# Attention products padded to 128 contracted rows, and transposes alternated with products of 64 columns, in a two-layer float32 encoder

## The chip, the cores and the metric

The kernel runs on one core of one Trainium2 chip. The metric is the device time of one execution in microseconds (us), median of several runs; lower is better. Engines are named as the profile names them: PE is TensorE's matmul, PEld its weight load, DVE is VectorE, ACT is ScalarE, POOL is GpSimd, SP is SyncE, which issues the transfers.

## What is computed

512 tokens of width 1024 in float32 go through two layers and a final RMS norm. Each layer is: norm, token mixer, residual; norm, squared-ReLU MLP of width 4096, residual; then a gated embedding added to the residual.

```python
# layer 0: three groups of five heads of width 64, windows of dilation 1, 4, 16;
# per head: s = q k^T * 64**-0.5, masked softmax, o = p v; the groups mixed by their log-sum-exp
x = x + dilated_window_mixer(rmsnorm(x), ...)
# layer 1: latent attention, 16 heads; q and k of width 64 + 32 (rotated), v of width 64
x = x + latent_attention_mixer(rmsnorm(x), ...)     # full softmax over 512 keys
# after each mixer
x = x + relu(rmsnorm(x) @ w_up)**2 @ w_down
x = x + sigmoid(rmsnorm(x) @ w_gate) * (p @ w_proj)
```

## The kernel before, in words

Activations lie transposed, features on the partitions and tokens on the free axis, tokens sorted by their residue mod 4, so that each class is one tile of 128 tokens. Every float32 product runs as three float32r passes over operands split in two, hi.hi + lo.hi + hi.lo; `mm3` (lines 162 to 164) issues the three, and `split` (169, 170) makes the two parts, hi on ACT and lo on DVE. Weights come in blocks of up to 128x1024, two or three blocks ahead, split in the same way (137, 138).

**Layer 0, attention.** `attnA(i)` (411 to 588) takes head i of each of the three groups. Groups 1 and 2 share one product of 128 rows, with zeros put into the halves of `kh` and `kl_` (319 to 322). Group 0 has q hi over q lo in `qq`, and k hi twice in `kk`, so that one product of 128 rows (line 448) gives hi.hi + lo.hi; the third pass, hi.lo, is line 449, which contracts only the 64 rows of `kl`. `values0` (523 to 533) multiplies v of group 0: 128-column products with [v hi | v lo] (529), 64-column ones (531), and at the end line 532, a product of 64 rows of zeros over 512 columns whose only use is to close the accumulation. `weave` puts the steps of the next head's projections (`qkv`), or of the output projection (`woA1`), among those of `attnA`. After the last head lines 611 to 619 add the last k-tiles of the output projection, per output tile five products of 512 columns, of which line 617 contracts 64 rows; then come the residual (284), and the norm's split (172, 173) and squares, with POOL adding the squares (235). The MLP's first products follow and need each of those splits.

**Layer 1, latent attention.** After the projections (717 to 785) the main loop (931 to 958) runs over 64 steps s; a step is one tile of 128 queries of one head. `where(s)` gives the pair of heads p, the pair of query tiles tp, the head j and the tile i. In a step: `normal(s+3)` scales the exponentials (reciprocal on DVE, product on POOL, 857), `turn(s)` transposes the softmax in four 128x128 transposes (864) and splits it, `scores(s+4)` makes three products over 96 rows (847, shown as 162 to 164) and then minimum (849) and exponential (850), and `values(s-3)` makes two products of 128 stationary columns (883: [v hi | v lo] over p hi) and two of 64 (882 or 886: v hi over p lo), with the output's copy, sum and split (894, 895, 897) at every fourth step. Projections of later heads (`prepK`, `prepQ`, `groupQ`, `groupV`) and half of the output projection (`woB(0)`) are spread over the steps. The bank, tile and order of each instruction come from a scheduler that follows the program's order as far as slots are free: 8 banks of PSUM, 24 slots for 128x1024 tiles (`unit`), 18 for 128x512 (`half`).

`q` of a pair lies in two tiles taken anew for each pair (824), `k` in two pairs of tiles held from line 785 on; only their first 96 partitions are written and read.

Of the kernel before, what the change touches and what calls it, by code (L numbers as in the profile page):

```python
"""Two-layer hybrid encoder trunk (dilated window attention, latent attention) on one core.

Activations live transposed, features on partitions and tokens on the free axis, the tokens
sorted by their residue mod 4, so that each residue class is one tile of 128 tokens.
Every float32 product runs as three float32r passes over operands split exactly in two:
hi = round12(v), lo = v - hi, and a.b = hi.hi + lo.hi + hi.lo.
"""
# [16 lines left out]
P = 128  # L24
S = 512
# [17 lines left out]
def _schedule():  # L43
    """Weight blocks in the order of use: (name, index) -> columns per partition."""
    out = []
    for i in range(GH):
        out += [(("qkv", i, b), 1024) for b in range(4)]
        if i == 0:
            out += [(("v0", b), n * 320) for b, n in enumerate((3, 3, 2))]
    out += [(("woA1", m), 768) for m in range(8)]  # L50
    out += [(("woA2", h), 1024) for h in range(2)]
    out += _mlp_blocks(0)
    out += [(("win", b), 832) for b in range(4)]
    out += [((n, 0), c) for n, c in (("uq", 768), ("ukv", 512))]
    for g in range(1, 4):
        out += [((n, g), c) for n, c in (("uq", 768), ("ukv", 512))]
    out += [(("woB", h, b), 1024) for h in range(2) for b in range(4)]
    out += _mlp_blocks(1)
    return out
# [18 lines left out]
def trunk(ctx: ExitStack, tc: tile.TileContext, xT, pT, cols, mask, tabs, wts, out):  # L78
# [37 lines left out]
    # ---- weights: fetched and split a few blocks before their use  # L116
# [9 lines left out]
    def fetch(key, pieces=1):  # L126
        """Brings a block in and splits it; by pieces, a step per piece."""
# [20 lines left out]
    # ---- activations and constants  # L148
# [11 lines left out]
    def mm3(out_, l, r, first, last):  # L160
        """out += l.T @ r, l and r (hi, lo) pairs."""
        T.matmul(out_, l[0], r[0], start=first, stop=False)  # L162
        T.matmul(out_, l[1], r[0], start=False, stop=False)  # L163
        T.matmul(out_, l[0], r[1], start=False, stop=last)  # L164

    def split(hi, lo, src, gain=None):
        """hi, lo <- src (times a column), exactly."""
# [8 lines left out]
    # ---- norms  # L176
    def preload(func):
        """Has ScalarE's table of func in place ahead of its first use."""
        t = small(1)
        A.activation(t, ones[:, :1], func)  # L180

    def rsqrt(ss, n, width):
        """1/sqrt(ss/width + eps) of n columns, a tile or one by one: three Newton steps."""
# [22 lines left out]
    def spread(r, n):  # L206
        """The n columns of r along the free axis of a bank, on all partitions."""
# [5 lines left out]
    class Norm:  # L213
        """Takes finished tiles of x: the gained tiles split, and the tokens' sums of squares."""
# [33 lines left out]
        def columns(self, blocks=False):  # L248
            """rstd of the tokens as [128, 4] columns, by classes, and then by blocks of 128."""
# [11 lines left out]
        def row(self):  # L261
            """The columns along the free axis, on all partitions."""
            rb = half()
            A.copy(rb, spread(self.r, NT))
            return rb

    def blocked(t, done=False):
        """t by blocks of 128 tokens (done: already laid out so), of each class 32."""
# [5 lines left out]
    def dense(key, kt, rhs, n=1, c0=0):  # L274
        """An output tile [128, 512] in PSUM, weights stationary."""
# [10 lines left out]
    def rope(E, t, heads, half, c0, s0):  # L286
        """Rotates the leading 2*half columns of each head of t [128, 4, heads, w] in place."""
# [15 lines left out]
    def weave(main, side, n_side, lead=0):  # L303
        """Emits side's n_side steps among those of main, which yields how far side should be (from the lead on)."""
# [13 lines left out]
    # ---- layer 0: dilated window attention  # L318
    kh, kl_ = unit(F32R, (P, NT, 256)), unit(F32R, (P, NT, 256))
    for t in (kh, kl_):  # L320
        G.memset(fl(t[0:64, :, 128:256]), 0.0)
        G.memset(fl(t[64:128, :, 0:128]), 0.0)

# [21 lines left out]
    # the tokens by blocks of 128: of each class the 32 from 32b  # L345
# [20 lines left out]
    def qkv(i):  # L366
        """q, k (roped) and v of head i of each group, tokens on partitions; not the v of group 0."""
# [44 lines left out]
    def attnA(i):  # L412
        qk, v12 = proj.pop(i)
        # q and k of head i of each group, transposed and split
# [9 lines left out]
        # group 0: queries by sixteens of each class, keys by thirty-twos  # L424
        qq, kk, kl = unit(F32R), half(F32R), half(F32R)
# [12 lines left out]
        # of both parts of the keys (group 0; groups 1 and 2), by query tiles: the least score, negated, and the sum  # L438
        st = small(16).rearrange("p (g t c) -> p g t c", g=2, t=NT)

        def scores(t):
            """Groups 1 and 2 for the class t, group 0 for 128 tokens from 128t+64 on (cyclically)."""
# [6 lines left out]
            T.matmul(ps[:, 256:], qq[:64, qs], kt(kl[:64]), start=False, stop=True)  # L449
# [9 lines left out]
        def mix():  # L459
            """The factors of both parts, by classes."""  # L460
# [30 lines left out]
        def turn0(ts):  # L491
            """Group 0 of query tiles; slots of the keys' block b: 2b, 2b + 1."""
# [7 lines left out]
        def turn(tp):  # L500
            """Groups 1 and 2 of two classes."""
# [7 lines left out]
        def values(tp):  # L509
            """o of groups 1 and 2 of two classes."""  # L510
# [12 lines left out]
        def values0():  # L523
            """o of group 0: [v hi | v lo] over p hi, v hi over p lo."""
# [3 lines left out]
            for b in (1, 3, 2, 0):  # L528
                T.matmul(out_(po, b), v0[b][:, i].rearrange("p z c -> p (z c)"), ph[:, 2 * b:2 * b + 2],
                         start=b == 1, stop=False)  # L530
                T.matmul(out_(po[:64], b), v0[b][:, i, 0, :], pl[:, 2 * b:2 * b + 2], start=False, stop=False)
            T.matmul(po, kh[:64, 0, P:], kh[:64, :, P:], start=False, stop=True)
# [29 lines left out]
        # group 0 by classes again, with its factors  # L562
# [29 lines left out]
    def woA1():  # L592
        """The output projection of the heads before the last ones."""
# [17 lines left out]
    for m in range(KD):  # L611
# [5 lines left out]
        T.matmul(ps, w[1][:64, c + P:c + 256], oA[7][0][:64], start=False, stop=True)  # L617
# [3 lines left out]
    # ---- squared-ReLU MLP, then the gated per-layer embedding  # L621
# [92 lines left out]
    # ---- layer 1: latent attention  # L714
# [6 lines left out]
    for tp in range(2):  # L721
# [10 lines left out]
        # the latent norms: columns (q, kv) of two token tiles, the scores' factor in q's, negated  # L732
# [16 lines left out]
    # the rotated key part in columns 64..95 of a slab of 128  # L749
# [11 lines left out]
    def groupQ(g):  # L761
        """q of four heads, roped, tokens on partitions; a step per token tile, then per product of the rotation."""
# [22 lines left out]
    kts = [(unit(F32R), unit(F32R)) for _ in range(2)]  # L785
# [6 lines left out]
    def groupV(g):  # L792
        """v of four heads, tokens on partitions: [hi | lo] of each head."""
# [15 lines left out]
    qts = {}  # L809

    def prepK(p):
        """k of a pair of heads, transposed and split; a step per head."""
# [9 lines left out]
    def prepQ(p):  # L822
        """q of a pair of heads, transposed and split; a step per head."""
        qh, ql = unit(F32R), unit(F32R)
        qts[p] = qh, ql
# [10 lines left out]
    def where(s):  # L836
        """Pair of heads, pair of token tiles, head of the pair, tile of the pair."""
        return s // 8, s // 2 % 2, s // 4 % 2, s % 2

    def scores(s):  # L840
        """A token tile of queries of a head against all keys: the exponentials and their sum."""
        p, tp, j, i = where(s)
        (qh, ql), (kh, kl) = qts[p], kts[p % 2]
# [3 lines left out]
        mm3(ps, (qh[:QW, c], ql[:QW, c]), (kh[:QW, js], kl[:QW, js]), True, True)  # L847
# [11 lines left out]
    def turn(s):  # L859
        """The softmax transposed and split."""  # L860
        e, i = es.pop(s)[0], s % 2
        pt = bank()
        for c in range(4):
            T.transpose(pt[:, tok(c)], e[:, tok(c)], ident)  # L864
        if i == 0:
# [4 lines left out]
    def values(s):  # L870
        """Half of the keys into the output of two token tiles of a head."""
# [6 lines left out]
        v = [vs[p // 2][c // 2][:, c % 2, h * P:(h + 1) * P] for c in range(4)]  # L878
        for c in (2 * i, 2 * i + 1):
            if c == 3:  # L880
                for d in (2, 3):
                    T.matmul(o_[:64], v[d][:, :64], pl[:, d, :], start=False, stop=False)
            T.matmul(o_, v[c], ph[:, c, :], start=c == 0, stop=c == 3)  # L883
            if c == 1:
                for d in (0, 1):
                    T.matmul(o_[:64], v[d][:, :64], pl[:, d, :], start=False, stop=False)
        if i == 1:
            del pts[s // 2]
# [42 lines left out]
    for s in range(N + 3):  # L931
        if s + 3 < N:
            scaled = normal(s + 3)
        if s < N:
            turn(s)
        if s + LA < N:
            scores(s + LA)
        if 3 <= s:
            values(s - 3)
# [25 lines left out]
    # ---- last gate and the final norm, half of the tokens after the other  # L965
# [4 lines left out]
    def finish(h, acc, xg):  # L970
        """The final norm of half h: the tokens' sums of squares, row, products and stores."""
# [16 lines left out]
    def evac(h, b, ps, acc, xg):  # L988
        """Gate, residual and squares of two tiles, by tiles where ps is two banks; then their final gain."""
# [65 lines left out]
def _arrange(inp):  # L1055
    """Lays the inputs out for the chip; the constants depend on shapes alone."""
# [6 lines left out]
    def feat(a):  # L1063
        """[S, n*128] -> [128, n*S], tokens permuted."""
# [9 lines left out]
    def tiles(w, rows, cols_):  # L1074
        """[rows, cols] of w as [128, rows/128, cols]."""
# [12 lines left out]
    def one(w, k0, m):  # L1088
        """An output tile, eight k-tiles: [128, 8, 128]."""
# [37 lines left out]
    # rope tables of the permuted tokens, cos and sin of either width  # L1127
# [6 lines left out]
    # group 0: query tile t holds the sixteens 2t+1 and 2t+2 (mod 8) of each class, by class;  # L1134
    # the keys' blocks are t and t+1 (0 and 3), each by classes
# [11 lines left out]
    # groups 1 and 2: the keys of the query's class  # L1147
# [25 lines left out]
```

## Time and profile before

| | us |
|---|---|
| median of 3 runs (lowest, highest) | 1290.01 (1289.76, 1292.22) |
| span of the profiled execution | 1287.7 |
| PE busy | 1260.0 (98%) |
| PEld busy | 1055.5 (82%) |
| DVE busy | 737.8 (57%) |
| ACT busy | 587.2 (46%) |
| POOL busy | 139.5 (11%) |
| mean granted TensorE clock | 0.994 |

The profile gives the span, from the first instruction to the last, of one execution; its own time is not listed apart from the runs, whose median is 2.3 us above the span. Busy times of PE are modelled from pipelined products, so what one product costs is read from one start to the next, and not from its duration. Layer 0's attention lies at about 20 to 247 us, the first MLP and gate up to about 655, the latent attention up to about 862, the second MLP and the end behind it.

### The profile page before, as it was taken

How to read it: one execution, taken by the hardware profiler on the slowest of the kernel's cores; microseconds unless marked ns; L12 is line 12 of the kernel's file. 1: busy time of each engine (PE TensorE's matmuls, PEld its weight loads, DVE VectorE, ACT ScalarE, POOL GpSimd, SP SyncE). 2: the span in 40 equal slices, each digit the busy share in tenths (PEclk: the TensorE clock that was granted, in tenths of full speed). 3: DMA queues.
4: the chain of work that ended last, by engine and by line, in shares of the span. 5: the costliest groups of instructions: out<-in, count | busy, mean ns of one | idle time of the engine just before them, and what ended most of it. 6: DMA issues, size and time to landing. Idle time of an engine off the chain costs nothing.

```text
span 1287.7 us, 16148 instructions
## 1 busy us (share of the span) xinstructions
PE 1260.0 (98%) x6229; PEld 1055.5 (82%) x6229; DVE 737.8 (57%) x1236; ACT 587.2 (46%) x967; POOL 139.5 (11%) x173
## 2 busy tenths in 40 slices
PE   8999999999999999999999999999999999999997
PEld 6877778688888888888888888888888888888896
DVE  7566666744343343454778999864434434335477
ACT  5555564543132231344458887754313313224464
POOL 5000000200000000011123443220000000000200
PEclk9999999899999999999999999999999999999998
DMA  6211112222222222232220010122332232223342
GB/s 222 67 66 66 58 50 94 79 84 96 98 98 98 98 98 98 98 112 88 87 74 26 30 40 27 34 84 96 99 98 98 98 98 96 92 96 110 99 155 108
DMA packets 34348, 113.18 MB, mean 88 GB/s; under 512 B 4064, under 2 KB 4832, under 8 KB 34272
## 3 DMA queue, kind: packets, MB, share of 16 engines
q1 hardware_dynamic: 34272, 112.15, 25.8%
q8 instruction: 49, 0.80, 0.3%
q14 instruction: 27, 0.22, 0.1%
HBM read 110.04 MB, written 2.10 MB: 87 GB/s over the span
## 4 chain that ended last, share of the span: by engine, by line
PE 85%; DVE 8%; ACT 5%; issue 1%; DMA 1%; POOL 0%; DVEq 0%; SPq 0%; ACTq 0%
PE ps L162 26%; PE ps L164 26%; PE ps L163 26%; PE ps L864 2%; DVE wl L138 1%; DVE u L173 1%; DVE x L284 1%; ACT u L169 1%; DVE u L170 1%; PE ps L883 1%; ACT h L850 1%; ACT h L169 1%; ACT wh L137 1%; PE ps L257 1%; PE ps L449 0%
## 5 line engine op out<-in xcount | busy, mean ns | idle before, releaser
L162 PE MATMUL ps<-u,wh 128*128 128x512 f32 (+1 forms) x1256 | 477.4, 380 | 2.1 <-ACT u L172 2.1
L164 PE MATMUL ps<-u,wh 128*128 128x512 f32 (+1 forms) x1256 | 476.8, 380 | 2.5 <-DVE u L173 2.5
L163 PE MATMUL ps<-u,wl 128*128 128x512 f32 (+1 forms) x1256 | 475.9, 379 | 0.0
L137 ACT CAST wh<-wr 128x1024 fp32r<-128x1024 f32 (+4 forms) x213 | 215.5, 1013 | 524.1 <-PE ps L164 454.1
L138 DVE TENSOR_TENSOR wl<-wr,wh 128x1024 fp32r<-128x1024 f32 (+4 forms) x213 | 252.4, 1186 | 95.3 <-ACT wh L137 94.9
L164 PEld LDWEIGHTS ps<-u,wh 128*128 128x128 f32 x1256 | 236.8, 189 | 48.5 <-DVE u L173 3.8
L162 PEld LDWEIGHTS ps<-u,wh 128*128 128x128 f32 x1256 | 236.8, 189 | 46.5 <-ACT u L172 2.7
L163 PEld LDWEIGHTS ps<-u,wl 128*128 128x128 f32 x1256 | 236.9, 189 | 43.9
L284 DVE TENSOR_TENSOR x<-x,ps 128x512 f32<-128x512 f32 x96 | 65.8, 686 | 179.8 <-PE ps L164 178.5
L235 POOL TENSOR_TENSOR h<-h,h 128x512 f32<-128x512 f32 x30 | 48.1, 1602 | 771.5 <-ACT h L234 767.7
L635 DVE SCALAR_TENSOR_TENSOR u<-ps,h 128x512 f32<-128x512 f32 x64 | 44.0, 691 | 135.6 <-PE ps L164 135.6
L162 PE MATMUL ps<-wh,u 128*128 128x512 f32 (+4 forms) x272 | 102.7, 382 | 6.6 <-ACT wh L137 5.5
L170 DVE TENSOR_TENSOR u<-ps,u 128x512 fp32r<-128x512 f32 (+4 forms) x148 | 96.3, 665 | 18.9 <-ACT u L169 17.5
L163 PE MATMUL ps<-wh,u 128*128 128x512 f32 (+4 forms) x272 | 99.5, 368 | 0.0
L164 PE MATMUL ps<-wl,u 128*128 128x512 f32 (+4 forms) x272 | 98.3, 368 | 0.3 <-DVE wl L138 0.3
L169 ACT CAST u<-ps 128x512 fp32r<-128x512 f32 (+4 forms) x148 | 81.2, 573 | 34.5 <-PE ps L505 14.1
L162 PEld LDWEIGHTS ps<-wh,u 128*128 128x128 f32 x272 | 51.4, 189 | 13.4 <-ACT wh L137 5.8
L170 DVE TENSOR_TENSOR u<-u,u 128x1024 fp32r<-128x1024 f32 x34 | 41.7, 1225 | 29.9 <-ACT u L169 29.9
L164 PEld LDWEIGHTS ps<-wl,u 128*128 128x128 f32 x272 | 51.2, 189 | 7.7 <-DVE wl L138 1.3
L163 PEld LDWEIGHTS ps<-wh,u 128*128 128x128 f32 x272 | 51.6, 190 | 6.3 <-issue 1.0
L857 POOL TENSOR_SCALAR h<-h,sm 128x512 f32<-128x512 f32 x64 | 44.7, 699 | 101.9 <-DVE sm L856 73.3
L162 PE MATMUL ps<-h,wh 128*128 128x512 f32 x120 | 49.0, 409 | 0.9 <-ACT h L169 0.8
(163 smaller groups left out, 1301.8 us busy)
## 6 DMA issues: line engine op xcount, KB each, us to landing
wr<-wts SPq DMA_DIRECT2D x182, 512.0 KB, 3.4
wr<-wts SPq DMA_DIRECT2D x12, 384.0 KB, 3.1
wr<-wts SPq DMA_DIRECT2D x12, 256.0 KB, 5.2
x<-xT SPq DMA_DIRECT2D x8, 256.0 KB, 5.8
wr<-wts SPq DMA_DIRECT2D x4, 416.0 KB, 3.2
out<-u SPq DMA_DIRECT2D x6, 256.0 KB, 2.1
u<-pT SPq DMA_DIRECT2D x2, 512.0 KB, 4.5
wr<-wts SPq DMA_DIRECT2D x2, 480.0 KB, 5.1
```

Of the source, the lines that this page charges most:

```text
L137: A.copy(hi[:, c], raw[:, c])
L138: V.tensor_tensor(lo[:, c], raw[:, c], fl(hi[:, c]), op=ALU.subtract)
L162: T.matmul(out_, l[0], r[0], start=first, stop=False)
L163: T.matmul(out_, l[1], r[0], start=False, stop=False)
L164: T.matmul(out_, l[0], r[1], start=False, stop=last)
L169: a = A.copy(hi, src)
L170: v = V.tensor_tensor(lo, src, fl(hi), op=ALU.subtract)
L235: (V if self.n == KD - 1 else self.eng).tensor_tensor(self.acc, self.acc, sq, op=ALU.add)
L284: V.tensor_tensor(x[m], x[m], src, op=ALU.add)
L635: V.scalar_tensor_tensor(u[:, j * S:(j + 1) * S], ps[j], 0.0, rb[0], op0=ALU.max, op1=ALU.mult)
L857: return G.tensor_scalar(e, e, rl, 1.0, op0=ALU.mult, op1=ALU.mult)
L864: T.transpose(pt[:, tok(c)], e[:, tok(c)], ident)
```

## The change

Three things. In layer 0, line 449 contracts 128 rows: `kl` becomes one of two tiles held through the layer, whose upper 64 rows are zeroed once by POOL; the closing product of line 532 is dropped; and line 617 contracts 128 rows, both halves of tile `oA[7]`, which holds hi over lo (so a product lo.lo is added). In the latent attention q and k contract 128 rows: q gets two pairs of tiles held from the start, and rows 96 to 127 of all eight q and k tiles are zeroed once by POOL. And the order in a step of the latent attention becomes: first `values(s-3)`'s product of 128 columns (two of them in even steps), then transpose, 64-column product, transpose, 64-column product, transpose, transpose, the last 128-column product (in odd steps), and only then `scores(s+4)`.

```diff
+    k0l = [half(F32R) for _ in range(2)]
+    for t in k0l:
+        G.memset(fl(t[64:128]), 0.0)
...
-        qq, kk, kl = unit(F32R), half(F32R), half(F32R)
+        qq, kk, kl = unit(F32R), half(F32R), k0l[i % 2]
...
-            T.matmul(ps[:, 256:], qq[:64, qs], kt(kl[:64]), start=False, stop=True)
+            T.matmul(ps[:, 256:], qq[:, qs], kt(kl), start=False, stop=True)
...
                 T.matmul(out_(po, b), v0[b][:, i].rearrange("p z c -> p (z c)"), ph[:, 2 * b:2 * b + 2],
-                         start=b == 1, stop=False)
-                T.matmul(out_(po[:64], b), v0[b][:, i, 0, :], pl[:, 2 * b:2 * b + 2], start=False, stop=False)
-            T.matmul(po, kh[:64, 0, P:], kh[:64, :, P:], start=False, stop=True)
+                         start=b == 1, stop=b == 0, skip_group_check=True)
+                T.matmul(out_(po[:64], b), v0[b][:, i, 0, :], pl[:, 2 * b:2 * b + 2], start=False, stop=b == 0,
+                         skip_group_check=True)
...
-        T.matmul(ps, w[1][:64, c + P:c + 256], oA[7][0][:64], start=False, stop=True)
+        T.matmul(ps, w[1][:, c + P:c + 256], oA[7][0], start=False, stop=True)
...
-    kts = [(unit(F32R), unit(F32R)) for _ in range(2)]
+    kts, qts = ([(unit(F32R), unit(F32R)) for _ in range(2)] for _ in range(2))
+    for t in sum(kts + qts, ()):
+        G.memset(fl(t[QW:]), 0.0)
...
-        qh, ql = unit(F32R), unit(F32R)
-        qts[p] = qh, ql
+        qh, ql = qts[p % 2]
...
-        mm3(ps, (qh[:QW, c], ql[:QW, c]), (kh[:QW, js], kl[:QW, js]), True, True)
+        mm3(ps, (qh[:, c], ql[:, c]), (kh[:, js], kl[:, js]), True, True)
...
         for c in range(4):
             T.transpose(pt[:, tok(c)], e[:, tok(c)], ident)
+            yield
...
-        for c in (2 * i, 2 * i + 1):
-            if c == 3:
-                for d in (2, 3):
-                    T.matmul(o_[:64], v[d][:, :64], pl[:, d, :], start=False, stop=False)
-            T.matmul(o_, v[c], ph[:, c, :], start=c == 0, stop=c == 3)
-            if c == 1:
-                for d in (0, 1):
-                    T.matmul(o_[:64], v[d][:, :64], pl[:, d, :], start=False, stop=False)
+        hi = lambda c: T.matmul(o_, v[c], ph[:, c, :], start=c == 0, stop=c == 3)
+        hi(2 * i)
+        if i == 0:
+            hi(1)
+        for c in (2 * i, 2 * i + 1):
+            yield
+            T.matmul(o_[:64], v[c][:, :64], pl[:, c, :], start=False, stop=False)
+        yield
         if i == 1:
+            hi(3)
...
-        if s < N:
-            turn(s)
+        tn, vl = turn(s) if s < N else iter(()), values(s - 3) if 3 <= s else iter(())
+        next(vl, None)
+        for _ in range(2):
+            next(tn, None)
+            next(vl, None)
+        run(tn)
+        run(vl)
         if s + LA < N:
             scores(s + LA)
-        if 3 <= s:
-            values(s - 3)
```

## Rows read from the trace of the kernel before

**Rows 1.** Busy time by stage: from and to in us, length, then busy us (instructions) of PE, PEld, DVE, ACT and POOL, the granted clock, the DMA engines' share and GB/s. Layer 0's attention; the wait for the norm behind it; the stretch after that wait; the latent attention's start; its main loop.
```profile
20.00:222.00 202.00, 198.20 (x1040) 162.62 (x1039) 129.65 (x316) 107.83 (x254) 24.08 (x40) 1.00 0.21 70
...
241.00:247.66 6.66, 3.88 (x15) 2.25 (x13) 6.66 (x7) 3.02 (x5) 3.03 (x2) 1.00 0.29 101
247.66:254.49 6.83, 6.62 (x20) 5.56 (x21) 4.16 (x15) 2.53 (x3) 0.00 (x0) 0.50 0.14 58
655.00:690.00 35.00, 31.79 (x175) 28.15 (x174) 27.18 (x81) 20.85 (x43) 4.59 (x9) 1.00 0.17 46
690.00:842.00 152.00, 150.20 (x959) 132.75 (x958) 136.44 (x266) 124.30 (x269) 58.96 (x82) 1.00 0.11 36
```

**Rows 2.** What PE waited for between 20 and 222 us: the waiting group, who released it, us in total, times, longest.
```profile
PE ps L418 <- DVE qk L296: 2.0, 3, 0.7
...
PE ps L449 <- DVE h L435: 0.6, 3, 0.2
```

**Rows 3.** Timeline of PE in layer 0's scores: start, us, then engine, line, operation, tiles, shape and count.
```profile
56.88 0.28 PE L448 MATMUL ps<-h,u 128*128 128x256 f32 x1
57.08 0.38 PE L449 MATMUL ps<-h,u 64*128 64x256 f32 x1
57.39 0.38 PE L162 MATMUL ps<-u,u 128*128 128x256 f32 x1
57.62 0.28 PE L163 MATMUL ps<-u,u 128*128 128x256 f32 x1
```

**Rows 4.** Timeline of PE at the end of `values0`, same columns.
```profile
70.56 0.28 PE L529 MATMUL ps<-u,u 128*128 128x256 f32 x1
70.68 0.28 PE L531 MATMUL ps<-u,u 128*64 128x256 f32 x1
70.89 0.49 PE L532 MATMUL ps<-u 64*128 64x512 f32 x1
71.31 0.50 PE L163 MATMUL ps<-wh,u 128*128 128x512 f32 x1
71.65 0.40 PE L164 MATMUL ps<-wl,u 128*128 128x512 f32 x1
```

**Rows 5.** Timeline of PE in the last part of layer 0's output projection, same columns.
```profile
228.47 0.39 PE L616 MATMUL ps<-h,wh 128*128 128x512 f32 x1
228.79 0.50 PE L617 MATMUL ps<-h,wl 64*128 64x512 f32 x1
229.22 0.50 PE L164 MATMUL ps<-h,wh 128*128 128x512 f32 x1
229.55 0.39 PE L616 MATMUL ps<-h,wh 128*128 128x512 f32 x1
```

**Rows 6.** Timeline of DVE in the same stretch and behind it; in brackets the idle time before the row and what ended it. The rows left out follow one another without idle time.
```profile
231.94 0.69 DVE L284 TENSOR_TENSOR x<-x,ps 128x512 f32<-128x512 f32 x1 [0.85 <-PE ps L617]
232.54 2.44 DVE L173 SCALAR_TENSOR_TENSOR u<-x,gains,u 128x512 fp32r<-128x512 f32 x2
...
246.06 2.41 DVE L173 SCALAR_TENSOR_TENSOR u<-x,gains,u 128x512 fp32r<-128x512 f32 x2
```

**Rows 7.** Timeline of PE in a step of the latent attention; rows of one form are merged, with their count.
```profile
821.95 0.60 PE L864 MATMUL ps<-ident,h 128*128 128x128 f32 x4
822.30 0.48 PE L162 MATMUL ps<-u,u 96*128 96x512 f32 x1
822.62 0.39 PE L163 MATMUL ps<-u,u 96*128 96x512 f32 x1
822.86 0.40 PE L164 MATMUL ps<-u,u 96*128 96x512 f32 x1
823.09 0.40 PE L883 MATMUL ps<-u,u 128*128 128x256 f32 x2
823.33 0.40 PE L886 MATMUL ps<-u,u 128*64 128x256 f32 x2
823.56 0.60 PE L864 MATMUL ps<-ident,h 128*128 128x128 f32 x4
```

**Rows 8.** The same in the last steps, where no scores are left and values follow the transposes.
```profile
838.32 0.60 PE L864 MATMUL ps<-ident,h 128*128 128x128 f32 x4
838.67 0.48 PE L883 MATMUL ps<-u,u 128*128 128x256 f32 x2
838.99 0.39 PE L886 MATMUL ps<-u,u 128*64 128x256 f32 x2
```

**Rows 9.** Weight loads by form: line, engine, operation, tiles, stationary shape, count | busy us, mean ns of one | idle before. The transposes of the softmax (864) load 128 columns, those of q (830) load 96.
```profile
L864 PEld LDWEIGHTS ps<-ident,h 128*128 128x128 f32 x256 | 30.7, 140 | 4.7 <-POOL h L857 0.5 <-issue 0.5
...
L830 PEld LDWEIGHTS ps<-ident,qk 128*96 128x96 f32 x64 | 7.2, 126 | 0.7 <-PE ps L164 0.5
```

**Rows 10.** Timeline of PE: eight transposes of q, one after the other.
```profile
682.79 1.05 PE L830 MATMUL ps<-ident,qk 128*96 128x128 f32 x8 [0.26 <-DVE qk L296]
```

**Rows 11.** Timeline of POOL: in layer 0's start, and around the start of the latent attention.
```profile
17.72 0.62 POOL L339 TENSOR_SCALAR h<-h 128x512 fp32r<-128x512 f32 x1 [14.18 <-DMA h<-tabs]
...
656.67 0.52 POOL L753 MEMSET u<- 128x512 f32 x1
...
675.51 0.60 POOL L296 TENSOR_TENSOR u<-u 128x64 f32<-128x64 f32 x2
691.71 0.69 POOL L857 TENSOR_SCALAR h<-h,sm 128x512 f32<-128x512 f32 x1 [15.59 <-PE ps L164]
```

**Rows 12.** Timeline of PE: the first product of scores in the latent attention.
```profile
684.08 0.50 PE L162 MATMUL ps<-u,u 96*128 96x512 f32 x1 [0.24 <-ACT u L169]
```

More of the change, by code (lines that the diff above doesn't have):

```diff
@@ L808, in trunk @@
     oB = [None] * 8
-    qts = {}
     def prepK(p):
@@ L842, in scores @@
         p, tp, j, i = where(s)
-        (qh, ql), (kh, kl) = qts[p], kts[p % 2]
+        (qh, ql), (kh, kl) = qts[p % 2], kts[p % 2]
         js = slice(j * S, (j + 1) * S)
```

## The prediction

> **What bounds the kernel now.** I read the busy times by stage first, then what PE waited for, then PE's timeline at each place that the change touches. In layer 0's attention PE is busy 198.20 of 202 us at full granted clock, DVE 129.65 and ACT 107.83 [rows 1]; PE's waits on single releasers are small, the largest being 2.0 us behind the rotation of q and k [rows 2]. So in this stage time on PE is time on the path. The exception is its end: between 241 and 247.66 us PE has 3.88 us of work and DVE is busy all of 6.66, so there DVE sets the pace, and the stretch behind it runs at a granted clock of 0.50, the lower of the two levels (1.2 of 2.4 GHz) [rows 1]. In the main loop of the latent attention PE is busy 150.20 of 152 us, but DVE 136.44 and ACT 124.30 beside it [rows 1]: PE leads, with little behind it.
>
> Products overlap, so a product's cost is the step from one start to the next. The reader should see two steps first: 0.23 us for 512 columns (822.86 to 823.09) and 0.12 for 256 (two in 823.09 to 823.33) [rows 7].
>
> **Products of 64 rows in layer 0.** They cost more than these steps, and so do their neighbours. In the scores, from L448 at 56.88 to the second product behind L449 at 57.62 is 0.74 us for three products of 256 columns that would take 0.36 at 0.12 each [rows 3]. The excess is 0.38: L448 waits longer for its successor (0.20), L449 takes 0.31, and the first product behind it 0.23. With 128 rows the neighbours match, and I take the excess as gone: 5 heads x 4 tiles x 0.38 = 7.6 us. The lower bound is half of it, if only the step on one side goes.
>
> The closing product L532 is dropped. From L531 at 70.68 to L164 at 71.65 is 0.97 us; without L532 there would be one of 256 columns and one of 512, 0.12 + 0.23 = 0.35 [rows 4]. 5 x 0.62 = 3.1 us.
>
> L617 has the same pattern: L616 to L616 is 1.08 us for three products of 512 columns, 0.69 at 0.23 each [rows 5]. 8 x 0.39 = 3.1 us of PE time. But behind these products DVE runs without a pause from 231.94 to 248.47, with residuals, norm splits and weight splits, and the MLP's first products wait for it [rows 6]. What PE saves here reaches the path only through DVE's one idle gap, 0.85 us before 231.94, which a product of this line ended [rows 6]. By that point three of the eight excesses (1.2 us) have been saved, so the whole gap can go: 0.85 us. The other 2.3 us become a longer wait of PE. The bounds are 0 and 3.1.
>
> The wait is followed by 6.83 us at half clock with 20 products in it [rows 1]. If the stretch were absent, half of it, 3.4 us, would be saved; if the longer wait brought a second one, 3.4 more would be lost. PE did 3.88 us of work in 6.66 before it fell, and it will do no more than that afterwards, so I leave the stretch as it is: 0, with both ends kept for the range.
>
> Is the rest of layer 0 able to follow? DVE uses 64% of this stage and ACT 53% [rows 1]. The stall behind the rotation does not move, since the last projection, the rotation and the five projection steps issued ahead of the transposes are untouched. The wait of L449 for DVE's lo part of k, 0.6 us [rows 2], stays. If the softmax chain became the bound, up to half of 10.7 us would be given back.
>
> **Padding 96 rows to 128.** The steps of the 96-row products are 0.24 and 0.23, and four transposes with the first of them take 0.67, which is 4 x 0.11 + 0.23 [rows 7]: nothing of the pattern of 64 rows is there. I take 0; from the rounding of these steps the bounds are 0.01 us a product either way, 192 x 0.01 = 1.9 us.
>
> The Trainium skill, page "TensorE: Matmul & The Clock Gate", section "Part 3: Packing small matmuls", speaks against padding: it says that a weight load overlaps products in flight only where its row group is another. By that rule full-height products would stop overlapping their loads, and none of the 7.6 us would come. The trace disagrees: full-height neighbours step at 0.23, and it is the 64-row product that steps at 0.43 (228.79 to 229.22) [rows 5].
>
> **Alternating transposes and 64-column products.** A step now has four transposes in a row, 0.11 us each ((0.60 - 0.27) / 3, taking 0.27 as one's own length, the time left at the end of the row), then later two 64-column products at 0.12 [rows 7]. Would pairing hide one under the other? Only if a transpose's pace were set by its weight load. Transposes that load 96 columns have shorter loads, 126 against 140 ns [rows 9], yet eight of them take 1.05 us, again 0.11 each [rows 10]. So the pace comes from the 128 columns streamed through, and these cannot hide under another product's columns. Nor does the boundary cost anything: four transposes and two 128-column products take 0.67 us (838.32 to 838.99), 4 x 0.11 + 2 x 0.12 [rows 8]; a 64-column product ahead of transposes steps at 0.12 [rows 7]. I take 0. The pair transpose, 64-column product is not in the trace, so the bounds are wide. Below: if the transposes' pace were half load and half streaming after all, 0.05 us of load each would hide, and as much of the product's load: 128 pairs x 0.06 = 7.7 us saved. Above: the excess of a 64-row product between full ones, 0.38 [rows 3].
>
> **The moved order.** Scores come four products of values later, 0.48 us, and on ACT and DVE the copy, sum and split of a finished output now stand ahead of the next minimum and exponential at every fourth step. The minimum feeds a softmax that is transposed four steps later, and a step is 152 us over some 65, about 2.3 us [rows 1]; nine microseconds cover it. Without that cover each such step would cost up to 2 us, since DVE is 90% busy. The transposes wait less for POOL's scaling, because a product goes ahead of them. q's fixed tiles were last read a pair earlier than they are rewritten, which adds no wait. No transfer is added or moved. I take 0, bounds 1 us either way.
>
> **The zeros.** A memset of 512 columns took 0.52 us [rows 11]. In layer 0 two of them join POOL's queue, which is idle for 14.18 us up to 17.72 [rows 11]. In layer 1 eight of 1024 columns make 8 x 1.04 = 8.3 us on POOL, which does nothing from 676.1 to 691.7 [rows 11]. Started at 676.1 they end at 684.4; the first scores, at 684.08 [rows 12], need four of them, the latest being the sixth at 682.3. Covered: 0. Should they have to wait for slots, or run ahead of POOL's rotation of k, up to 8.3 us would show.
>
> **The sum.** 7.6 + 3.1 + 0.85 = 11.55 us. The span before, 1287.7, becomes 1276.2; with the 2.3 us by which the median lies over it, 1278.5 us.
>
> **The rivals.** (a) *The pairs overlap*: a transpose and a 64-column product hide part of each other. For it: no row shows the pair; both loads are shorter than those of full products. Against: the pace of the 96-column transposes. 1278.5 - 7.7 = 1270.8.
>
> (b) *Slower, by drained pairs*: a 64-column product standing alone between transposes makes PE run empty on both sides, as a 64-row one does. Its place is the loop's 64 steps, two products in each; its price at the excess of rows 3 is 128 x 0.38 = 48.6 us, giving 1327. From 11.55 / 128 = 0.09 us a product on it outweighs all gains. Against it: 128- and 64-column products follow one another at 0.12, and so do 64-column products and transposes [rows 7]. The Trainium skill, page "TensorEngine Tiling (Array Packing)", sections "Key Properties" and "Restrictions", has this rule: changing the tiling mode drains TensorE, and column tiling excludes the fp32 transpose mode. For rows the trace agrees, with 0.38; for 64 columns it shows no such cost so far.
>
> (c) *Layer 0 does not follow*: the softmax chain takes over and half of 10.7 is given back, 1283.8.
>
> (d) *The zeros or the new order stall the latent attention*: up to 8.3 us back, 1286.8; half of that is the likelier size, 1282.6.
>
> (e) *The change does not do what it says*: the scheduler issues by its own order, and the pairs may not alternate. As I cost them at 0, the time stays 1278.5.
>
> **How the numbers follow.** Forecast, with (e) in it: 0.68, own range 1275 to 1282 (the clock's 3.4 us either way). (a) 0.14, (b) 0.04, (c) 0.08, (d) 0.06. The range from 1270 to 1283.5 takes in (a) to its full size, and leaves out (b), about half of (c) and (d), and a few cases in which a gain of (a) meets one of the clock. A change of 0.2%, 2.6 us, is about what measurement tells here; slower by that needs (b) or a stall over 14 us: 0.04. Within 0.2%: 0.03. Faster: 0.93.
>
> **What would show it.** Right: L449 and L617 at steps of 0.12 and 0.23 with ordinary neighbours; L532 gone; layer 0's attention shorter by about 10.7 us up to the last head; PE's wait before the MLP longer by about 2; the main loop of the latent attention near 152 us at full clock; POOL's zeros ending before the first scores. Wrong: a shorter main loop with transpose and 64-column product together under 0.23 us would be (a); steps over 0.12 at the 64-column products (b); new waits of PE on DVE or ACT between 50 and 222 us (c); PE waiting on POOL near 684 (d).

## The result and the profile after

After the change the median is 1282.73 us (four runs, 1280.75 to 1284.43), against 1290.34 for the kernel before beside it: a ratio of 0.9937, 95% interval 0.9923 to 0.9951. The change gains 7.6 us of the 11.55 forecast. The sign and the range held; the median lies 4.2 us over the predicted 1278.5.

Where the gain arose is seen from marks that every trace has: the end of the first head's rotation of q and k, the MLP's first residual, the gate's first one, the first exponential of the latent attention, the ninth residual of its output projection (the first wholly behind the loop), and the end of the span. The table gives the us between them, for the profiled executions of the kernels before and after, and of four experiments that are told below.

| | before | after | layer 0 part only | zeros only | zeros early | 128 rows, no alternation |
|---|---|---|---|---|---|---|
| to the first rotation | 49.5 | 50.8 | 49.8 | 49.8 | 49.9 | 50.2 |
| to the MLP's first residual | 259.2 | 249.4 | 248.8 | 259.2 | 248.9 | 249.0 |
| to the gate's first residual | 316.0 | 316.1 | 316.0 | 316.0 | 316.1 | 316.1 |
| to the first latent exponential | 63.0 | **65.8** | 63.0 | **65.4** | 63.1 | **65.2** |
| to the ninth latent residual | 159.3 | 159.9 | 159.3 | 160.4 | 159.6 | 160.0 |
| rest | 440.7 | 440.6 | 440.7 | 440.8 | 440.6 | 440.6 |

Marks are read to 0.1 us, so an entry can be 0.1 off. The first line varies by a microsecond between executions of any kernel, and the profiled execution after was the slowest of its four (1284.43 us, span 1282.6). So the profiles show only 5.1 us of the 7.6. The columns are read below their first line: the stage with layer 0's attention gained 9.8 us, and 2.8 came back ahead of the latent attention's first exponential.

First PE's timeline after, at the places of [rows 3, 4, 5 and 7] (start, us, engine, line, operation, tiles, shape, count; L449 is now L454, L532 is gone, L617 is L622, the transposes are L870 and the products of 128 and 64 columns L886 and L892).
```profile
58.44 0.28 PE L453 MATMUL ps<-h,u 128*128 128x256 f32 x1
58.56 0.28 PE L454 MATMUL ps<-h,u 128*128 128x256 f32 x1
58.68 0.40 PE L162 MATMUL ps<-wh,u 128*128 128x512 f32 x1
...
70.64 0.28 PE L536 MATMUL ps<-u,u 128*64 128x256 f32 x1
70.76 0.40 PE L163 MATMUL ps<-wh,u 128*128 128x512 f32 x1
70.99 0.40 PE L164 MATMUL ps<-wl,u 128*128 128x512 f32 x1
...
88.41 0.28 PE L453 MATMUL ps<-h,u 128*128 128x256 f32 x1
88.86 0.39 PE L454 MATMUL ps<-h,u 128*128 128x256 f32 x1 [0.17 <-DVE h L440]
89.08 0.40 PE L162 MATMUL ps<-wh,u 128*128 128x512 f32 x1
89.32 0.40 PE L163 MATMUL ps<-wh,u 128*128 128x512 f32 x1
...
227.02 0.39 PE L621 MATMUL ps<-h,wh 128*128 128x512 f32 x1
227.25 0.39 PE L622 MATMUL ps<-h,wl 128*128 128x512 f32 x1
227.48 0.39 PE L162 MATMUL ps<-h,wh 128*128 128x512 f32 x1
...
812.08 0.27 PE L870 MATMUL ps<-ident,h 128*128 128x128 f32 x1
812.11 0.36 PE L892 MATMUL ps<-u,u 128*64 128x256 f32 x1
812.31 0.27 PE L870 MATMUL ps<-ident,h 128*128 128x128 f32 x1
...
812.99 0.39 PE L163 MATMUL ps<-u,u 128*128 128x512 f32 x1
813.22 0.40 PE L164 MATMUL ps<-u,u 128*128 128x512 f32 x1
```
The reader should see steps. L453 to L454 to L162: 0.12 each, where 0.20 and 0.31 stood. L536 to L164: 0.35, where it was 0.97. L621 to L622 to L162: 0.23 each. A pair of transpose and 64-column product takes 0.23 us (812.08 to 812.31), a transpose's 0.11 and a product's 0.12. The padded products still step at 0.23 (812.99 to 813.22). Only L453 to L454 at 88.41 is long, 0.45, because L454 waits there for DVE.

Then busy time by stage after (columns as in [rows 1]): the wait ahead of the MLP, the stretch behind it, the stall before the latent scores, the stretch behind that, the main loop.
```profile
230.24:236.90 6.66, 3.90 (x14) 2.05 (x12) 6.66 (x7) 3.21 (x6) 4.01 (x3) 1.00 0.23 79
236.90:247.13 10.23, 8.74 (x25) 7.20 (x26) 5.79 (x17) 2.97 (x4) 0.89 (x1) 0.50 0.31 103
670.00:673.80 3.80, 1.61 (x10) 0.99 (x9) 2.38 (x10) 2.14 (x5) 3.80 (x5) 1.00 0.00 0
673.80:680.63 6.83, 6.08 (x20) 4.52 (x21) 6.25 (x13) 4.92 (x10) 1.14 (x2) 0.50 0.00 0
685.00:838.00 153.00, 150.89 (x965) 134.41 (x964) 136.05 (x266) 124.03 (x267) 58.08 (x82) 1.00 0.11 36
```
The main loop is as dense as before (150.89 of 153 us at full clock). What is new is the third line: PE has 1.61 us of work in 3.80 us, POOL is busy in all of them, and then the granted clock falls to 0.50, the lower of the two levels (1.2 of 2.4 GHz), for 6.83 us in which the kernel before ran at full clock.

What POOL does there, from its timeline:
```profile
667.69 7.25 POOL L793 MEMSET u<- 32x1024 f32 x8
```
And DVE's timeline beside it, the columns of the latent norm:
```profile
667.76 1.79 DVE L192 TENSOR_SCALAR sm<-sm 128x4 int32<-128x4 int32 x1
669.59 0.16 DVE L200 TENSOR_TENSOR sm<-sm 128x4 f32<-128x4 f32 x1
...
669.98 0.16 DVE L202 SCALAR_TENSOR_TENSOR sm<-sm,sm 128x4 f32<-128x4 f32 x1
...
671.36 0.90 DVE L746 TENSOR_SCALAR sm<-sm 128x2 f32<-128x2 f32 x1
```
The zeros ended at 674.94, in time for the first scores. But two steps of four and two columns took 1.79 and 0.90 us. The same two steps, L192 and L741, took 0.17 each before:
```profile
676.25 0.17 DVE L192 TENSOR_SCALAR sm<-sm 128x4 int32<-128x4 int32 x1
...
678.22 0.17 DVE L741 TENSOR_SCALAR sm<-sm 128x2 f32<-128x2 f32 x1
```
The excess is 1.62 + 0.73 = 2.35 us on a chain that ACT, and behind it PE, waits for. After the change:
```profile
671.36 0.69 ACT L762 ACTIVATE u<-z,sm 128x128 f32<-128x128 f32 x2 [2.15 <-DVE sm L202]
...
674.55 0.79 PE L162 MATMUL ps<-u,wh 128*128 128x512 f32 x1 [2.12 <-ACT u L172]
```
Before, ACT's wait for the same line L202 was 0.53 us and PE's wait 1.32. A memset takes 7.25 / 8 = 0.91 us, so the second step stood for one of them, the first for about two. Both are TENSOR_SCALAR. The TENSOR_TENSOR and SCALAR_TENSOR_TENSOR steps between them kept their 0.16 under the same memsets.

### The profile page after: what moved, and what is told of

Read it like the earlier page. It is cut to its first block, busy times and chain, and to the rows that moved or that the text cites. A ratio compares the mean times of both kernels' runs of the same rounds, so it can differ in the third digit from the quotient of the medians.

```text
span 1282.6 us, 16154 instructions
## 1 busy us (share of the span) xinstructions
PE 1252.5 (98%) x6224; PEld 1057.6 (82%) x6224; DVE 738.5 (58%) x1236; ACT 586.7 (46%) x967; POOL 147.8 (12%) x183
## 4 chain that ended last, share of the span: by engine, by line
PE 85%; DVE 8%; ACT 5%; issue 1%; DMA 1%; DVEq 0%; SPq 0%; ACTq 0%
PE ps L164 26%; PE ps L162 26%; PE ps L163 26%; PE ps L870 2%; DVE wl L138 1%; DVE x L284 1%; PE ps L892 1%; DVE u L173 1%; PE ps L886 1%; DVE u L170 1%; ACT wh L137 1%; ACT h L169 1%; ACT u L169 1%; ACT u L172 1%; PE ps L257 1%
## 5 line engine op out<-in xcount | busy, mean ns | idle before, releaser
L164 PE MATMUL ps<-u,wh 128*128 128x512 f32 (+1 forms) x1256 | 478.0, 381 | 3.4 <-DVE u L173 3.4
L162 PE MATMUL ps<-u,wh 128*128 128x512 f32 (+1 forms) x1256 | 478.1, 381 | 3.0 <-ACT u L172 3.0
L163 PE MATMUL ps<-u,wl 128*128 128x512 f32 (+1 forms) x1256 | 476.9, 380 | 0.0
L164 PEld LDWEIGHTS ps<-u,wh 128*128 128x128 f32 x1256 | 237.2, 189 | 49.9 <-DVE u L173 5.2
L162 PEld LDWEIGHTS ps<-u,wh 128*128 128x128 f32 x1256 | 237.3, 189 | 47.4 <-ACT u L172 3.5
L163 PEld LDWEIGHTS ps<-u,wl 128*128 128x128 f32 x1256 | 237.2, 189 | 44.2
L162 PE MATMUL ps<-wh,u 128*128 128x512 f32 (+4 forms) x272 | 102.7, 382 | 6.2 <-ACT wh L137 5.5
L163 PE MATMUL ps<-wh,u 128*128 128x512 f32 (+4 forms) x272 | 100.0, 370 | 0.0
L164 PE MATMUL ps<-wl,u 128*128 128x512 f32 (+4 forms) x272 | 99.2, 371 | 0.3 <-DVE wl L138 0.3
L169 ACT CAST u<-ps 128x512 fp32r<-128x512 f32 (+3 forms) x148 | 81.7, 572 | 29.8 <-PE ps L510 11.6
L162 PEld LDWEIGHTS ps<-wh,u 128*128 128x128 f32 x272 | 52.2, 192 | 12.2 <-ACT wh L137 5.8
L164 PEld LDWEIGHTS ps<-wl,u 128*128 128x128 f32 x272 | 51.9, 191 | 7.7 <-DVE wl L138 1.3
L163 PEld LDWEIGHTS ps<-wh,u 128*128 128x128 f32 x272 | 52.2, 192 | 6.0 <-DVE u L173 0.3
L870 PE MATMUL ps<-ident,h 128*128 128x128 f32 x256 | 51.0, 272 | 0.3 <-ACT h L856 0.2
```

The costliest lines, as they stand in the source:

```text
L169: a = A.copy(hi, src)
```

## The experiments

The theory to be tested: layer 0 gives the whole gain, padding and alternation nothing, and the zeros, where they stand in POOL's order, cost some 2.7 us. The rivals: that padded products or the alternation cost it, and that layer 0 gave less than its sum.

**The change cut in four.** All ran beside the kernel before at 1290.93 us. The layer 0 part only is the diff down to L622, without the rest:
```
-    kts, qts = (...)                  +    kts = [(unit(F32R), unit(F32R)) for _ in range(2)]
-        G.memset(fl(t[QW:]), 0.0)     (q's tiles, products, order of steps: as before)
```


> Only layer 0's part of the change (lines 449, 532, 617); the latent attention as before. Theory Z (the eight memsets of the latent attention's zeros delay DVE's small steps beside them, PE waits, and its clock falls): 1290.3 - 8.4 = 1281.9 us, with the start of the latent scores some 63 us behind the last residual of layer 0's MLP, as before, against 65.8 in the changed kernel, and no half clock near 674 us; faster than the changed kernel's slow profile by 2 to 3 us. Rival P (the latent part as a whole costs nothing and layer 0 simply gains 7.6): 1282.7, the same as the whole change. My own sum of before: 1278.7.

Measured 1279.93 us, ratio 0.9916 (0.9902 to 0.9929): 11.0 us gained. Of the sum of 11.55 nearly all is there, and the change as a whole is 2.8 us slower than this part alone. So layer 0 followed, and something else costs.

Layer 0 and alternation, products over 96 rows, no zeros:
```
-    for t in sum(kts + qts, ()):
-        G.memset(fl(t[QW:]), 0.0)
...  (q in tiles taken anew for each pair, as before)
-        mm3(ps, (qh[:, c], ql[:, c]), (kh[:, js], kl[:, js]), True, True)
+        mm3(ps, (qh[:QW, c], ql[:QW, c]), (kh[:QW, js], kl[:QW, js]), True, True)
```


> The whole change without the latent attention's zeros and with its products over 96 rows again; alternation kept. Theory Z: the start of the latent attention is as before (63 us), the main loop 0.6 us longer than before: 1282.5 or less. Rival A (the moved order costs it): as long as the whole change, 1282.7, with the start still late.

Measured 1280.21, ratio 0.9919 (0.9906 to 0.9933): 0.3 us from the kernel without alternation, inside both intervals. The alternation costs and gains nothing that can be measured.

Layer 0, zeros and 128 rows, the order of transposes and products as before:

> The whole change without the alternation: transposes in a row, scores ahead of values, as before; zeros and 128 rows kept. Theory Z: start of the latent attention late by 2.8 us as in the changed kernel, main loop as before: 1282 to 1284.7. Rival A: start as before, 1279.

Measured 1283.04, ratio 0.9939 (0.9927 to 0.9951), the time of the whole change. What costs is therefore in the padding, and it is one of two things: the products over 128 rows or their zeros.

The zeros alone, on the kernel before: fixed tiles for q and the eight memsets, with rows that no product reads.
```
+    kts, qts = ([(unit(F32R), unit(F32R)) for _ in range(2)] for _ in range(2))
+    for t in sum(kts + qts, ()):
+        G.memset(fl(t[QW:]), 0.0)
...
-        qh, ql = unit(F32R), unit(F32R)
+        qh, ql = qts[p % 2]
...
```


> The kernel before, with the fixed q tiles and the eight memsets added and nothing else; the products still read 96 rows, so the zeros are never read. Theory Z: slower than before by 2 to 6 us (the delay of DVE's small steps, and half clock where it follows): 1292.5 to 1296. Rival P: 1290.3, no change, since POOL has nothing else to do there.

Measured 1293.55, ratio 1.0022 (1.0013 to 1.0031): 2.6 us slower than the kernel before, with no product changed. POOL in this kernel:
```profile
676.47 7.25 POOL L787 MEMSET u<- 32x1024 f32 x8
```
and DVE:
```profile
676.55 1.79 DVE L192 TENSOR_SCALAR sm<-sm 128x4 int32<-128x4 int32 x1
...
680.15 0.90 DVE L741 TENSOR_SCALAR sm<-sm 128x2 f32<-128x2 f32 x1
```
The same two steps with the same lengths. This rules out the padded products as the cause. That q's tiles are now held could still matter; the kernel with early zeros, next, holds them too.

**The zeros in other places.** Three kernels, beside 1290.0 us for the kernel before. The whole change with the same eight memsets emitted ahead of q's norm split, so that POOL runs them before the last norm chain:
```
+    kts, qts = (...); for t in sum(kts + qts, ()): G.memset(fl(t[QW:]), 0.0)
     qTh, qTl = unit(F32R), unit(F32R)
     ...
-    (the same lines behind the split of cT)
```


> The whole change with the eight memsets asked for ahead of the latent transposes, so that POOL runs them in its idle time before the rotation of k, beside the first norm chain (which has some 3 us to spare) and not beside the last. Theory L: 1280.2 to 1281.5. Rival (POOL's work as such delays the latent attention): 1282.7 or more.

Measured 1280.39, ratio 0.9920 (0.9907 to 0.9932). POOL and DVE:
```profile
646.92 7.27 POOL L750 MEMSET u<- 32x1024 f32 x8
```
```profile
666.66 0.17 DVE L192 TENSOR_SCALAR sm<-sm 128x4 int32<-128x4 int32 x1
668.64 0.17 DVE L746 TENSOR_SCALAR sm<-sm 128x2 f32<-128x2 f32 x1
```
Run 20 us earlier, with the padded products and q's held tiles kept, the same memsets cost nothing that can be measured: the steps are back at 0.17, and the time to the first latent exponential at 63.1 us. This is the cause, shown by moving it.

The early memsets do hold up DVE. They run beside the first norm chain, whose same lines took 0.16 or 0.17 each in the whole change:
```profile
650.90 0.58 DVE L190 TENSOR_SCALAR sm<-sm 128x4 f32<-128x4 f32 x1
...
651.52 0.89 DVE L192 TENSOR_SCALAR sm<-sm 128x4 int32<-128x4 int32 x1
```
L189, which reads from PSUM, kept its 0.16 beside them. PE's waits between 640 and 670 us are those of the layer 0 part, 0.7 and 0.4 us, so no time is lost. It is the slack of the chain beside them that makes the zeros free here, and not the absence of small steps.

Sixty-four memsets of 128 columns in place of eight of 1024, unread, on the kernel before:
```
-        G.memset(fl(t[QW:]), 0.0)
+        for c in range(0, 1024, 128):
+            G.memset(fl(t[QW:, c:c + 128]), 0.0)
```


> zeros_only with each memset of 1024 columns cut into eight of 128: the same bytes and at least the same time on POOL, in pieces of some 0.1 us in place of 0.91. Theory L: a step of DVE waits for one piece at most, 0.2 us over the chain: 1290.6 to 1291.3. Rival (POOL's busy time beside DVE is what counts): 1293.5 as zeros_only, or more.

Measured 1291.59, ratio 1.001 (1.0001 to 1.0019). POOL and DVE:
```profile
678.01 9.48 POOL L788 MEMSET u<- 32x128 f32 x64
```
```profile
678.08 0.29 DVE L192 TENSOR_SCALAR sm<-sm 128x4 int32<-128x4 int32 x1
...
680.19 0.27 DVE L741 TENSOR_SCALAR sm<-sm 128x2 f32<-128x2 f32 x1
```
A memset now takes 9.48 / 64 = 0.15 us, and the steps wait 0.12 and 0.10 instead of 1.62 and 0.73, although POOL is busy for longer. What counts is the length of one memset, not their sum. Of the 2.6 us some 1.6 are left. By the marks of the profiled execution, the time to the first latent exponential is 63.4 us, 0.4 more than before (2.4 more with the zeros only): 0.2 are the steps, and a stretch of 3.41 us at half clock at 684 lies in it too. Another 1.0 us lies behind it, 160.4 us to the ninth residual, as with the zeros only. Both kernels hold q's tiles; so does the one with early zeros, at 159.6. What lengthens that stage was not tested and stays open.

The whole change with the zeros brought by eight transfers on SP's queue:
```
+    none = cp.tile([P - QW, P], F32)
-        G.memset(fl(t[QW:]), 0.0)
+        nc.sync.dma_start(out=fl(t[QW:]).rearrange(...), in_=none.unsqueeze(1).to_broadcast(...))
```


> The whole change, but the zeros of the eight latent tiles come by eight transfers on SP's queue from a 32x128 tile zeroed at the start, so that POOL has no memset beside DVE's small steps. Theory L (DVE's two-scalar steps of the norm chain stand still until the memset running on POOL ends): 1280.2, as without zeros; L192 and L746 back at 0.17 us each, no half clock near 674 us. Rival P (the products over 128 rows cost it): 1282.7 as the whole change.

Measured 1283.92, ratio 0.9950 (0.9937 to 0.9962): the expectation missed by 3.7 us. DVE and PE:
```profile
666.58 0.17 DVE L194 TENSOR_SCALAR sm<-sm 128x4 int32<-128x4 int32 x1
```
```profile
675.70 0.79 PE L164 MATMUL ps<-u,u 128*128 128x512 f32 x1 [1.51 <-ACT u L171]
...
678.22 0.79 PE L165 MATMUL ps<-u,u 128*128 128x512 f32 x1 [0.88 <-DVE u L172]
```
The time alone would speak for rival P; the early zeros, with the same products, speak against it. The first step, now L194, is at 0.17, as expected, and so is the second, so no memset means no stall. But ACT and DVE now run splits of 32 rows, those of the second pair's rotated key part, ahead of q's; PE waits 1.51 and 0.88 us for them, and 675.33 to 682.16 runs at 0.50. Another order by the scheduler has taken the stall's place. Why it chose this order was not tested.

**The parts of layer 0.** Beside 1290.62 us. L449 over 128 rows (with its zeros), L532 dropped, L617 over 128 rows, each alone on the kernel before:

> The kernel before with line 449 over 128 rows and nothing else. My forecast: 20 products x 0.38 = 7.6 us off 1290.9, 1283.3. Rival (the softmax chain takes over): half, 1287.1.

> The kernel before without the closing product of line 532 and nothing else. My forecast: 5 x 0.62 = 3.1 us off, 1287.8. Rival (only its own step counts, 0.42 x 5, and its neighbours stay slow for another reason): 1288.8.

> The kernel before with line 617 over 128 rows and nothing else. My forecast: DVE sets the pace there, so 0.85 us off, 1290.0, and PE waits some 2.3 us more before the MLP; the half clock may last longer and take up to 1.7 us of it back. Rival (PE sets the pace): 3.1 off, 1287.8.

Measured 1284.54 (ratio 0.9955, 0.9942 to 0.9968), 1288.13 (0.9978, 0.9969 to 0.9987) and 1290.32 (0.9997, 0.9988 to 1.0005): gains of 6.1, 2.5 and 0.3 us. The third cannot be told from nothing. In the profiled executions the stage up to the MLP's first residual, 259.2 us before, became 253.1, 256.1 and 257.3: 6.1, 3.2 and 1.9 us less. For line 617 the profile and the median differ, and the granted clock differs with them: seven of its eleven executions had a mean clock of 0.991 and took 1290.3 to 1291.8 us, the other four, the profiled one among them, 0.994 and 1289.1 to 1289.7. The expectation had named a longer half clock as what could take the gain back; no profile of such an execution was kept. As the three together gave 11.0, it was taken away from them:
```
-        T.matmul(ps, w[1][:, c + P:c + 256], oA[7][0], start=False, stop=True)
+        T.matmul(ps, w[1][:64, c + P:c + 256], oA[7][0][:64], start=False, stop=True)
```


> Layer 0's part without line 617: lines 449 and 532 alone, the latent attention as before. If the single parts add up (6.1 and 2.5 us off) and DVE sets the pace at line 617: 1282.0 against 1290.6, with the half clock before the MLP at 6.83 us as before. If line 617 gives more once PE arrives earlier: 1282 too, but then layer0_only's 1279.9 is line 617's doing, some 2 us. If line 617 only lengthens PE's wait and the half clock: 1279.9 or less.

Measured 1281.95 beside 1290.66, ratio 0.9935 (0.9921 to 0.9948), 2.0 us behind the three together, though the intervals overlap. DVE's timeline without this line:
```profile
223.99 0.69 DVE L284 TENSOR_TENSOR x<-x,ps 128x512 f32<-128x512 f32 x1 [0.87 <-PE ps L622]
224.59 2.44 DVE L173 SCALAR_TENSOR_TENSOR u<-x,gains,u 128x512 fp32r<-128x512 f32 x2
```
and with it (layer 0 part only):
```profile
220.81 1.96 DVE L284 TENSOR_TENSOR x<-x,ps 128x512 f32<-128x512 f32 x3
222.68 1.49 DVE L173 SCALAR_TENSOR_TENSOR u<-x,gains,u 128x512 fp32r<-128x512 f32 x2
```
The gap of 0.87 is gone, as forecast, and the first two norm splits take 1.49 in place of 2.44. DVE's chain from the first residual of this stretch to the end of the last norm split is 17.1 us with the line (from 220.81) and 18.8 without it (from 221.74): 1.7 less, of which the gap is half. The other half is what is left of splits that are shorter at first and longer later (the fifth and sixth take 3.46 in place of 2.44), and of a shorter weight split. POOL's additions begin at 223.99, at the end of the first two splits, with the line, and at 224.91, inside the first of them, without it; that splits are longer beside them is likely from the traces, but was not tested by itself.

**A 64-row product put where there was none.** The layer 0 part, with the third pass of the latent scores over 64 rows (k's lo part of the rotated columns is left out of the scores):
```
...  (the first two passes over 96 rows, as before)
+        T.matmul(ps, qh[:64, c], kl[:64, js], start=False, stop=True)
```


> Layer 0's part of the change, and in the latent attention the third pass of the scores (q hi over k lo) contracts 64 rows in place of 96: k lo's rotated part is left out of the product. Theory R (a product of 64 rows between taller ones makes PE run empty on both sides, whatever its place): 64 x 0.39 = 25 us more than layer0_only, 1305. Rival S (fewer rows cost nothing, and what layer 0 lost at these lines came from their place): 1279.9.

Measured 1299.76, ratio 1.0070 (1.0058 to 1.0083): 19.8 us over the layer 0 part, 0.31 for each of 64 products; the expectation was 25 us. Its PE timeline:
```profile
790.37 0.48 PE L853 MATMUL ps<-u,u 96*128 96x512 f32 x1
790.68 0.40 PE L854 MATMUL ps<-u,u 96*128 96x512 f32 x1
791.01 0.49 PE L855 MATMUL ps<-u,u 64*128 64x512 f32 x1
791.43 0.50 PE L891 MATMUL ps<-u,u 128*128 128x256 f32 x2
791.77 0.40 PE L894 MATMUL ps<-u,u 128*64 128x256 f32 x2
```
The product of 96 rows is left after 0.33 instead of 0.23, the one of 64 takes 0.42, and the two of 256 columns behind it 0.34 instead of 0.24. These steps add up to 0.39 a product, as expected, where the runs give 0.31; where the rest went was not worked out. The pattern of [rows 3] appears in another stage as soon as one product has 64 rows, and 96 rows next to 128 show nothing of it. The Trainium skill, page "TensorEngine Tiling (Array Packing)", section "Key Properties", says that a change of the tiling mode drains TensorE. For rows this trace agrees, with 0.39 us here; for the 64 columns of L892 between transposes the trace after shows none, 0.23 for the pair.

## Why the forecast was right in sign and 4 us too large

**Products of 64 rows.** The pattern was read rightly: every excess was taken back on both sides. The term of 7.6 us was mis-sized. It multiplied one tile's excess by twenty. In the three middle heads the first tile's L449 waited for DVE, and still does. PE in the kernel before, at the place of 88.41 above:
```profile
89.08 0.28 PE L448 MATMUL ps<-h,u 128*128 128x256 f32 x1
89.53 0.38 PE L449 MATMUL ps<-h,u 64*128 64x256 f32 x1 [0.17 <-DVE h L435]
89.83 0.50 PE L162 MATMUL ps<-wh,u 128*128 128x512 f32 x1
90.17 0.39 PE L163 MATMUL ps<-wh,u 128*128 128x512 f32 x1
```
L448 to L163 was 1.09 us. It is 0.91 now (88.41 to 89.32): 0.18 saved, not 0.38. In the fourth tile of each head, where transposes follow, 0.33 are saved. By the steps: 12 x 0.38 + 3 x 0.18 + 5 x 0.33 = 6.75 us; alone it measured 6.1, with 7.6 just outside its interval of 4.1 to 7.5. The prediction had named this wait as staying (0.6 us, [rows 2]) and not taken it out of the product.

**L532** was right: the step 0.97 to 0.35 is as worked out (3.1 us; 2.5 measured, and 3.1 is inside its interval of 1.7 to 4.0; 3.2 by the marks).

**L617**: 0.85 forecast as DVE's gap. The gap closed. Beside the others it is worth about 2.0 us, alone 0.3, both within measurement of 0.85; the bounds of 0 to 3.1 held. By the marks it is 1.4 (248.8 us to the MLP's first residual, against 250.2 without it) to 1.9, more than the gap, because DVE's chain got shorter too. So this chain was not as fixed as the prediction had it. With this line alone PE's waits for the norm splits grew by 1.2 us (from 3.0 to 4.2), not by the 2.3 forecast.

**The half clock ahead of the MLP** was left as it is. It became 10.23 us, from 6.83, after PE had done 3.90 us of work in 6.66. The kernels with the whole layer 0 part that ended best have the longer stretch too, and without L617 it is 6.83. Half of the 3.4 added microseconds is at most 1.7 us of PE's time, inside the 11.0 measured.

**Padding and alternation at 0** held. The latter's pair takes 0.23 us, and rivals (a) and (b) both fall with it: a gain would show it under 0.23, a drain well over.

**Layer 0 does not follow**, rival (c), did not come: 11.0 of 11.55.

**The zeros, "Covered: 0", is the step that failed.** It looked at when the memsets would end, and POOL was indeed done before the scores. It did not ask who runs beside them. Two DVE steps of the norm stood for 2.35 us, PE had 1.61 us of work in 3.80 meanwhile, and behind that the granted clock fell from 1.00 to 0.50. Rival (d) had the place and half its size (1282.6 against 1282.73), but another mechanism: not PE waiting on POOL, and not the moved order. That the numbers agree is luck. The Trainium skill, page "SBUF — State Buffer", section "Who interferes with whom", has the rule: VectorE and GpSimd share a pair of ports, held for a whole instruction, which tensor_scalar can want, and which tensor_tensor does not want beside an operation that only writes. The traces agree, with 1.79 and 0.90 us for TENSOR_SCALAR beside a memset and 0.16 for TENSOR_TENSOR; that the first step stood for two memsets the page does not say.

The sum by what was measured: 11.0 for layer 0, less 2.8 for the zeros, is 8.2; the whole measured 7.6, and the 0.6 between them is within the runs' scatter. Of the 11.55, then, about 0.5 is missing in layer 0, where L617 makes up for part of the mis-sized product, and 2.8 went with the zeros. The best version is the layer 0 part alone, 1279.93 us; padding with early zeros (1280.39) and 96 rows with alternation (1280.21) cannot be told from it.

## What to carry to other kernels

An excess read at one place is multiplied only by the places where the same neighbours stand and no other wait is already there; look at the first and last of each group. Work put on an idle engine is free only if nobody on the path shares a resource with it: look at what the neighbours run during its whole time, not only at when it ends. Clear padding long before the stage that uses it, beside a chain that has slack.

## What the runs showed of the hardware that was not expected

Beside memsets on POOL, DVE's steps of two and four columns took 0.90 and 1.79 us, against 0.17 undisturbed; with memsets cut into pieces of 0.15 us they took 0.27 and 0.29. A product of 64 rows among taller ones cost 0.31 us on average in two places where PE sets the pace (6.1 us for 20 in layer 0, 19.8 for 64 in the latent scores). Products of 64 columns and transposes alternated at no cost that can be measured.
